# Low parts of weights, reciprocal roots and their neighbours in VectorE's queue

## The chip, the cores and the metric

The kernel runs on one core of a Trainium2 chip. TensorE (PE) multiplies, ScalarE (ACT), VectorE (DVE) and GpSimd (POOL) do the elementwise work, SyncE (SP) issues the transfers. Each engine takes its instructions in one fixed order and waits on semaphores for the others. The metric is the device time of one execution in microseconds (us); of several runs the median stands.

## The reference

Three transformer-like blocks follow each other on one sequence of 512 tokens with 1024 channels, all in float32. Cut to what the change touches:

```
x = first_block(x, ...)     # pooling mixer, LN; dilated attention, LN
x = second_block(x, ...)    # rmsnorm; short conv, sparse attention, gMLP; rmsnorm, residual
x = third_block(x, ...)     # rmsnorm; gated linear attention + conv; rmsnorm; conv FFN; rmsnorm

def layer_norm(x, g, b):    # first block
    return (x - mean(x)) * rsqrt(var(x) + LN_EPS) * g + b

def hybrid_layer(x, ...):   # end of the second block
    out = rmsnorm(merged @ w_out, g_post)
    return x + gate * out

def mixer_merge(o_hg, g, ...):            # third block
    o = rmsnorm_3(o_hg, gn_w) * silu(g)   # per head of 128 channels
    y_hg = o @ w_hg_out
    u = silu(layernorm_3(dwconv1d(u, dw_w, dw_b), ln_w, ln_b))   # the conv norm
    y_cv = u @ w_cv_out
```

## The kernel before, in words

Activations lie channels by tokens: eight tiles of 128 channels by 512 tokens. A float32 product is made of three matmuls on split operands. `w()` (lines 123 to 131) loads a weight tile `wr` of 128x1024 by DMA, ACT copies its high part `wh` (line 129), and an elementwise subtraction gives the low part `wl` (line 130). `prod_a` then runs, for each of eight k, high by high, high by low and low by high (lines 143 to 145). The pool of weight tiles holds three of each kind. The attribute `wlo` says which engine makes the low part; it is set to POOL ahead of several places and back to DVE behind them.

`rsqrt` (lines 209 to 233) computes a reciprocal root by a bit trick and two steps of refinement on a tile of 128x4. On DVE it has ten instructions; with `eng` set to POOL the first one is on DVE and thirteen follow on POOL, since POOL makes each fused step (line 216) from two (lines 219 and 220). Nine roots pass POOL: the layer norm at the end of block 1 and the eight heads of the gated linear attention (gla) in block 3. `bcast_tok` (line 250) spreads a root over 128 partitions by four PE transposes, named `S`.

A scheduler orders each engine's instructions when the kernel is built, from priorities and estimated costs; `high_priority(offset=FIRST)` puts instructions ahead of the others that are ready. The order in the program is then fixed.

The places that matter:

- *End of block 1* (lines 642 to 664): layer norm root on POOL, then a sum of squares on PE, a second root on DVE (`rms_end`), and the modulation into `h2`. Beside it block 3's 256 context tokens are prepared (`cx`, scans at line 1065, transposes `T` at line 1075).
- *End of block 2* (lines 952 to 995): three sums over channels (`sum`, lines 290 and 967) are reduced by matmuls with ones (line 297); a first root, a few small steps `rs_v`, a second root; then per channel tile `acc` times the first root (line 985), plus the residual (line 986), stored, and in a second loop modulated with the second root into `h3`.
- *The gla heads* (`gla_back`, lines 1203 to 1222): output matmuls `O` (1207 to 1209), squares on ACT, a root on POOL, `o` = output times root (1215), four PE transposes `T` (1220).
- *The conv norm* (lines 1301 to 1314): statistics, a root on DVE, then per tile minus mean (1310), times root (1311), SiLU, split. Between them stand the products with `w_hg_out` (line 1307).
- *The halves* (line 322 on): the norm in front of the FFN, done for two halves of the tokens, with sums of squares `ss` (line 290) reduced at line 297.

Of the kernel before, what the change touches and what calls it, by code (L numbers as in the profile page):

```python
# [44 lines left out]
CPOOL = 1  # L45
# [8 lines left out]
class K:  # L54
    def __init__(self, ctx, tc, I):
        self.tc, self.nc, self.I = tc, tc.nc, I
        self.tasks, self.cols = [], {}
        self.wlo = self.nc.vector
        ep = ctx.enter_context
        self.const = ep(tc.tile_pool(name="const", bufs=1))  # L60
        self.wp = ep(tc.tile_pool(name="wp", bufs=3))
        self.big = ep(tc.tile_pool(name="big", bufs=6))
        self.wk = ep(tc.tile_pool(name="wk", bufs=2))
        self.sm = ep(tc.tile_pool(name="sm", bufs=3))
        self.mmp = ep(tc.tile_pool(name="mmp", bufs=3, space=PSUM))
# [57 lines left out]
    def w(self, src, kt, n=P, offset=None):  # L123

        with self.tc.high_priority(offset=offset):
            r = self.wraw(src, kt, n)
            h = self.wp.tile([P, kt, n], F32R, name="wh", tag="wh")
            l = self.wp.tile([P, kt, n], F32R, name="wl", tag="wl")
            self.nc.scalar.activation(h, r, AF.Copy)  # L129
            self.wlo.tensor_sub(l, r, h.bitcast(F32))  # L130
        return h, l
# [77 lines left out]
    def rsqrt(self, v, n, mult, eps, eng=None):  # L209

        e = eng or self.nc.vector

        def fma(out, a, b, y):

            if eng is None:
                e.scalar_tensor_tensor(out, a, b, y, op0=ALU.add, op1=ALU.mult)
            else:
                u = self.small((P, n), "rs_u", bufs=2)
                e.tensor_scalar(u, a, b, 0.0, op0=ALU.add, op1=ALU.add)
                e.tensor_mul(out, u, y)  # L220
        x, y, a, t, xc = (self.small((P, n), "rs_" + c, bufs=2) for c in "xyatc")
        self.nc.vector.tensor_scalar(x, v, mult, eps, op0=ALU.mult, op1=ALU.add)
        e.tensor_scalar(y.bitcast(I32), x.bitcast(I32), -0.5, float(0x5F3759DF), op0=ALU.mult, op1=ALU.add)

        e.tensor_mul(a, y, y)
        e.tensor_scalar(xc, x, -0.5 * 0.375 ** 3, 0.0, op0=ALU.mult, op1=ALU.add)  # L226
        e.tensor_mul(a, a, x)
        fma(t, a, -10.0 / 3, a)
        fma(y, t, 5.0, y)
        e.tensor_mul(a, y, y)  # L230
        e.tensor_mul(a, a, xc)
        fma(y, a, 1.5 * 0.375, y)
        return y
# [27 lines left out]
    def ln_end(self, st, eps, eng=None):  # L261

        mv = self.small((P, NT, 2), "mv4", bufs=1)
        for n in range(NT):
            self.nc.vector.bn_aggr(mv[:, n], st[:, n])
        m = self.bcast_tok(mv[:, :, 0])
        return m, self.bcast_tok(self.rsqrt(mv[:, :, 1], NT, 1.0, eps, eng))
# [52 lines left out]
    def halves(self, src, add, norms, finish, cut, mix):  # L320


        for j in range(cut):
            add(j)
        self.wlo = self.nc.gpsimd
# [84 lines left out]
def block1(k, ctx, w0, acc, x):  # L410
# [6 lines left out]
    for half in range(2):  # L417
        z = None
        for g in (2 * half, 2 * half + 1):
            w = POOL_W[g]  # L420
            k.wlo = nc.gpsimd if g == 1 else nc.vector
# [111 lines left out]
def block1b(k, ctx, acc, h1, x2d):  # L533
# [10 lines left out]
    for j in range(8):  # L544
        k.wlo = nc.gpsimd if j == 0 else nc.vector
# [8 lines left out]
        k.wlo = nc.vector  # L554
# [98 lines left out]
    mean, rstd = k.ln_end(st, LN_EPS, nc.gpsimd)  # L653
# [9 lines left out]
    k.wlo = nc.gpsimd  # L663
# [54 lines left out]
def block2(k, ctx, hT, x2d, x3d):  # L718
# [69 lines left out]
    k.wlo = nc.gpsimd  # L788
    kg = blocks("k"), blocks("v")
    k.wlo = nc.vector  # L790
# [177 lines left out]
    k.wlo = nc.gpsimd  # L968
# [13 lines left out]
    h = k.b16(F32R, name="h3h"), k.b16(F32R, name="h3l")  # L982
    for j in range(8):
        a = acc[:, j]
        nc.vector.tensor_mul(a, a, r)
        nc.vector.tensor_add(a, a, res[:, j])
        nc.sync.dma_start(out=x3d[:, j], in_=a)
    for j in range(8):
        k.modulate(j, acc[:, j], r2, k.cols["A3"], k.cols["B3"], h)
# [134 lines left out]
def gla_back(k, h, hT, V, R, q, tot, masks, gnw, DB, y):  # L1124
# [89 lines left out]
    r = k.rsqrt(ss, NT, 1.0 / P, EPS, nc.gpsimd)  # L1214
# [10 lines left out]
def block3(k, hT, x3d, out):  # L1225
# [49 lines left out]
    k.wlo = nc.gpsimd  # L1275
    run(BEFORE[:5])
    k.wlo = nc.vector
# [22 lines left out]
    k.wlo = nc.vector  # L1300
    yT = k.b16(name="yT")
    mean, rstd = k.ln_end(bst, EPS)
    yc = k.b16(F32R, name="ycvh"), k.b16(F32R, name="ycvl")
    for j in range(8):
# [5 lines left out]
        nc.vector.tensor_sub(c, c, mean)  # L1310
# [40 lines left out]
    for c0, nk in CHUNKS:  # L1351
        ft = k.b16(F32R, shape=(P, 2, 4, S), name="ft")
        for jj in range(nk):
# [14 lines left out]
            if j == CPOOL:  # L1368
                k.wlo = nc.vector
# [169 lines left out]
```

## Time and profile before

| | us |
|---|---|
| median of 3 runs (lowest, highest) | 3197.41 (3193.45, 3418.14) |
| the profiled execution, its own time | 3195.51 |
| its span, first to last instruction | 3193.5 |
| PE busy | 3090.1 (97%) |
| DVE busy | 2052.4 (64%) |
| ACT busy | 1242.9 (39%) |
| POOL busy | 310.8 (10%) |

The busy shares are means over stages with different limits. PE is nearly always busy, so what counts for an edit is whether PE waits at its place, and for whom. The views used are the page's shares, the waits grouped by who ended them, the granted TensorE clock by stretches, and the timelines of single places. A bracket at a timeline row's end gives the idle time before it and who ended it. A tile's name stands without its number, and `x4` at the end of a row means four such instructions in a row.

### The profile page before, as it was taken

What the parts mean: (1) busy time and instruction counts of PE and PEld (TensorE: products, weight loads), DVE (VectorE), ACT (ScalarE), POOL (GpSimd) and SP (SyncE); (2) the same over time, 40 slices, a digit from 0 to 9 for tenths busy, and PEclk for the clock granted to TensorE, in tenths of its full rate; (3) what the DMA queues carried; (4) which work ended last, traced back from release to release, by engine and by line L of the source; (5) the groups of instructions that cost most, each with busy time, mean ns of one, the idle gap of its engine ahead of it and who ended that gap; (6) DMA issues with size and microseconds to landing.
All of it is one profiled execution on the core that took longest, in us unless ns stands there. A gap on an engine that the chain in (4) does not pass through costs nothing.

```text
span 3193.5 us, 44907 instructions
## 1 busy us (share of the span) xinstructions
PE 3090.1 (97%) x17460; PEld 2547.2 (80%) x17460; DVE 2052.4 (64%) x4049; ACT 1242.9 (39%) x2092; POOL 310.8 (10%) x380
## 2 busy tenths in 40 slices
PE   8999999999999899999999999989999998989998
PEld 7888878787877787877778888878877776878886
DVE  8466664656454745555444354589997899688777
ACT  4333544434343433334443223342455462333232
POOL 1400000000000301111100101030010020210000
PEclk9999999999999999999999999999999999999999
DMA  8223343434322421111113222333222224422332
GB/s 289 100 93 132 114 160 112 152 114 146 123 87 71 129 99 66 60 66 66 54 57 106 93 92 93 134 120 112 98 91 69 90 73 142 139 73 93 98 100 80
DMA packets 112773, 334.41 MB, mean 105 GB/s; under 512 B 17584, under 2 KB 22704, under 8 KB 112560
## 3 DMA queue, kind: packets, MB, share of 16 engines
q1 hardware_dynamic: 112560, 331.54, 30.6%
q8 instruction: 137, 2.24, 0.3%
q14 instruction: 76, 0.62, 0.1%
HBM read 316.82 MB, written 14.68 MB: 104 GB/s over the span
## 4 chain that ended last, share of the span: by engine, by line
PE 45%; DVE 6%; ACT 2%; issue 1%; POOL 1%; DVEq 0%; ACTq 0%; POOLq 0%
PE mm L143 12%; PE mm L144 12%; PE mm L145 12%; PE O L885 1%; PE mm L172 1%; PE mm L174 1%; PE mm L173 1%; DVE wl L130 1%; PE S L869 1%; PE T L878 1%; DVE cy L1255 0%; ACT wh L129 0%; PE S L1161 0%; POOL rs_c L226 0%; DVE ss L290 0%
## 5 line engine op out<-in xcount | busy, mean ns | idle before, releaser
L129 ACT ACTIVATE wh<-wr 128x1024 fp32r<-128x1024 f32 (+3 forms) x505 | 504.4, 1000 | 1090.5 <-PE mm L144 823.6
L130 DVE TENSOR_TENSOR wl<-wr,wh 128x1024 fp32r<-128x1024 f32 (+2 forms) x455 | 547.7, 1205 | 436.6 <-ACT wh L129 433.1
L143 PE MATMUL mm<-h2h,wh 128*128 128x512 f32 (+1 forms) x776 | 309.5, 399 | 0.9 <-ACT th L677 0.8
L145 PE MATMUL mm<-h2h,wl 128*128 128x512 f32 (+1 forms) x776 | 309.3, 399 | 0.0
L144 PE MATMUL mm<-h2l,wh 128*128 128x512 f32 (+1 forms) x776 | 309.1, 398 | 0.0
L144 PE MATMUL mm<-h1l,wh 128*128 128x512 f32 x512 | 210.9, 412 | 1.7 <-DVE h1l L318 1.4
L143 PE MATMUL mm<-h1h,wh 128*128 128x512 f32 x512 | 207.0, 404 | 0.6 <-ACT h1h L317 0.6
L145 PE MATMUL mm<-h1h,wl 128*128 128x512 f32 x512 | 207.5, 405 | 0.0
L143 PE MATMUL mm<-h3h,wh 128*128 128x512 f32 x512 | 201.8, 404 | 3.4 <-ACT th L1261 2.2
L144 PE MATMUL mm<-h3l,wh 128*128 128x512 f32 x512 | 201.0, 402 | 1.5 <-DVE h3l L318 1.5
L145 PE MATMUL mm<-h3h,wl 128*128 128x512 f32 x512 | 199.7, 400 | 0.0
L1255 DVE SCALAR_TENSOR_TENSOR cy<-uc,dww,cy 128x512 f32<-128x512 f32 x240 | 177.1, 749 | 3.4
L143 PEld LDWEIGHTS mm<-h2h,wh 128*128 128x128 f32 (+1 forms) x776 | 145.8, 188 | 27.6 <-ACT th L677 1.5
L144 PEld LDWEIGHTS mm<-h2l,wh 128*128 128x128 f32 (+1 forms) x776 | 145.8, 188 | 26.2
L145 PEld LDWEIGHTS mm<-h2h,wl 128*128 128x128 f32 (+1 forms) x776 | 145.7, 188 | 25.3
L130 POOL TENSOR_TENSOR wl<-wr,wh 128x1024 fp32r<-128x1024 f32 (+1 forms) x50 | 118.3, 2370 | 324.7 <-ACT wh L129 324.6
L366 DVE CUSTOM_DVE_ANT_0 gr<-gr,crow 128x256 f32<-128x256 f32 x352 | 135.7, 440 | 9.5 <-DMA gr<-in_w_mod 6.3
L143 PE MATMUL mm<-h4h,wh 128*128 128x512 f32 (+1 forms) x368 | 140.6, 384 | 0.2 <-DVE fc L1366 0.2
L145 PE MATMUL mm<-h4h,wl 128*128 128x512 f32 (+1 forms) x368 | 140.7, 383 | 0.0
L144 PE MATMUL mm<-h4l,wh 128*128 128x512 f32 (+1 forms) x368 | 140.7, 383 | 0.0
L1363 DVE SCALAR_TENSOR_TENSOR fc<-up,fdw,fc 128x512 f32<-128x512 f32 x176 | 131.9, 751 | 4.9
L875 ACT ACTIVATE pe<-sb,nm 128x128 f32<-128x128 f32 (+3 forms) x128 | 71.3, 557 | 119.1 <-DVE nm L872 118.9
(522 smaller groups left out, 7283.9 us busy)
## 6 DMA issues: line engine op xcount, KB each, us to landing
gr<-in_w_mod SPq DMA_DIRECT2D x64, 512.0 KB, 4.8
wr<-in_w_up SPq DMA_DIRECT2D x44, 512.0 KB, 3.5
wr<-in_w_in_a SPq DMA_DIRECT2D x32, 512.0 KB, 3.5
wr<-in_w_f SPq DMA_DIRECT2D x32, 512.0 KB, 3.5
wr<-in_w_v SPq DMA_DIRECT2D x32, 512.0 KB, 3.7
wr<-in_w_in_b SPq DMA_DIRECT2D x32, 512.0 KB, 3.5
wr<-in_w_a SPq DMA_DIRECT2D x32, 512.0 KB, 3.5
gr<-in_w_ada SPq DMA_DIRECT2D x24, 512.0 KB, 4.5
```

What stands on the lines that cost most here:

```text
L129: self.nc.scalar.activation(h, r, AF.Copy)
L130: self.wlo.tensor_sub(l, r, h.bitcast(F32))
L143: mm(ps, lhsT=wh[:, k], rhs=xh[:, k0 + k, tok], start=first and k == 0, stop=False)
L144: mm(ps, lhsT=wh[:, k], rhs=xl[:, k0 + k, tok], start=False, stop=False)
L145: mm(ps, lhsT=wl[:, k], rhs=xh[:, k0 + k, tok], start=False, stop=last and k == kt - 1)
L172: mm(ps, lhsT=sel(xh, k), rhs=wh[:, kk], start=st, stop=False)
L173: mm(ps, lhsT=sel(xh, k), rhs=wl[:, kk], start=False, stop=False)
L174: mm(ps, lhsT=sel(xl, k), rhs=wh[:, kk], start=False, stop=en)
L366: nc.vector.tensor_tensor_reduce(out=r[:, sl], in0=r[:, sl], in1=self.crow[:, sl], scale=1.0, scalar=0.0, op0=ALU.mult, op1=ALU.add, accum ...
L875: nc.scalar.activation(pe, sb, AF.Exp, bias=m, scale=-1.0, accum_out=lt[:, n, b:b + 1])
L1255: nc.vector.scalar_tensor_tensor(c, u[:, t:t + S], dww[:, j, t:t + 1], c, op0=ALU.mult, op1=ALU.add)
L1363: nc.vector.scalar_tensor_tensor(c, u[:, a:a + 8, b:b + 64], fw[:, j, t:t + 1], c, op0=ALU.mult, op1=ALU.add)
```

## The change

All low parts are made on DVE: 50 move there from POOL (20 in block 1's pooling mixer and one in its halves, 10 in the stage around the end of block 1, 12 at the end of block 2, 7 before and in the FFN's start). All reciprocal roots run on DVE, in a section of highest priority, and so do the statistics' last step in `ln_end`. At two places `issue_after` queues passes over whole tiles behind the last instruction of a root, `k.chain`: the products of `acc` with the first root at the end of block 2, behind the second root, and the subtraction of the mean in the conv norm. The two loops at the end of block 2 become one.

```diff
@@ w()
             self.nc.scalar.activation(h, r, AF.Copy)
-            self.wlo.tensor_sub(l, r, h.bitcast(F32))
+            self.nc.vector.tensor_sub(l, r, h.bitcast(F32))
@@ rsqrt
-    def rsqrt(self, v, n, mult, eps, eng=None):
...
+    def rsqrt(self, v, n, mult, eps):
+
+        e = self.nc.vector
         x, y, a, t, xc = (self.small((P, n), "rs_" + c, bufs=2) for c in "xyatc")
...
+        fma = lambda out, a, b, y: e.scalar_tensor_tensor(out, a, b, y, op0=ALU.add, op1=ALU.mult)
+        with self.tc.high_priority(offset=FIRST):
+            e.tensor_scalar(x, v, mult, eps, op0=ALU.mult, op1=ALU.add)
+            e.tensor_scalar(y.bitcast(I32), x.bitcast(I32), -0.5, float(0x5F3759DF), op0=ALU.mult, op1=ALU.add)
+
+            e.tensor_mul(a, y, y)
+            e.tensor_scalar(xc, x, -0.5 * 0.375 ** 3, None, op0=ALU.mult)
+            e.tensor_mul(a, a, x)
+            fma(t, a, -10.0 / 3, a)
+            fma(y, t, 5.0, y)
+            e.tensor_mul(a, y, y)
+            e.tensor_mul(a, a, xc)
+            self.chain = fma(y, a, 1.5 * 0.375, y)
         return y
@@ ln_end
-        for n in range(NT):
-            self.nc.vector.bn_aggr(mv[:, n], st[:, n])
+        with self.tc.high_priority(offset=FIRST):
+            for n in range(NT):
+                self.nc.vector.bn_aggr(mv[:, n], st[:, n])
@@ end of block 1
-    mean, rstd = k.ln_end(st, LN_EPS, nc.gpsimd)
+    mean, rstd = k.ln_end(st, LN_EPS)
@@ end of block 2
     h = k.b16(F32R, name="h3h"), k.b16(F32R, name="h3l")
+    chain = k.chain
     for j in range(8):
         a = acc[:, j]
-        nc.vector.tensor_mul(a, a, r)
+        with k.tc.issue_after(chain.ins):
+            nc.vector.tensor_mul(a, a, r)
         nc.vector.tensor_add(a, a, res[:, j])
         nc.sync.dma_start(out=x3d[:, j], in_=a)
-    for j in range(8):
         k.modulate(j, acc[:, j], r2, k.cols["A3"], k.cols["B3"], h)
@@ gla_back
-    r = k.rsqrt(ss, NT, 1.0 / P, EPS, nc.gpsimd)
+    r = k.rsqrt(ss, NT, 1.0 / P, EPS)
@@ conv norm
     mean, rstd = k.ln_end(bst, EPS)
+    chain = k.chain
...
-        nc.vector.tensor_sub(c, c, mean)
+        with k.tc.issue_after(chain.ins):
+            nc.vector.tensor_sub(c, c, mean)
```

What the scheduler makes of it shows in the order of the instructions. Three places on DVE follow; a row is line, operation, output and inputs, shape.

DVE at the end of block 2, from the second root's first step `rs_x` on (`acc` is the channel tile, `S` the broadcast first root, `x2r` the residual). Before:

```order
L222 TENSOR_SCALAR rs_x<-rs_v 128x4
L986 TENSOR_TENSOR acc_17018<-acc_17018,x2r 128x512
L223 TENSOR_SCALAR rs_y<-rs_x 128x4
L226 TENSOR_SCALAR rs_c<-rs_x 128x4
L985 TENSOR_TENSOR acc_17018<-acc_17018,S 128x512
L225 TENSOR_TENSOR rs_a<-rs_y 128x4
L985 TENSOR_TENSOR acc_17018<-acc_17018,S 128x512
L227 TENSOR_TENSOR rs_a<-rs_a,rs_x 128x4
L986 TENSOR_TENSOR acc_17018<-acc_17018,x2r 128x512
L216 SCALAR_TENSOR_TENSOR rs_t<-rs_a 128x4
L986 TENSOR_TENSOR acc_17018<-acc_17018,x2r 128x512
L216 SCALAR_TENSOR_TENSOR rs_y<-rs_t,rs_y 128x4
```

Now (line 971 is the product of line 985 before):

```order
L213 TENSOR_SCALAR rs_x<-rs_v 128x4
L214 TENSOR_SCALAR rs_y<-rs_x 128x4
L217 TENSOR_SCALAR rs_c<-rs_x 128x4
L216 TENSOR_TENSOR rs_a<-rs_y 128x4
L128 TENSOR_TENSOR wl<-wr,wh 128x1024
L218 TENSOR_TENSOR rs_a<-rs_a,rs_x 128x4
L211 SCALAR_TENSOR_TENSOR rs_t<-rs_a 128x4
L211 SCALAR_TENSOR_TENSOR rs_y<-rs_t,rs_y 128x4
L221 TENSOR_TENSOR rs_a<-rs_y 128x4
L222 TENSOR_TENSOR rs_a<-rs_a,rs_c 128x4
L211 SCALAR_TENSOR_TENSOR rs_y<-rs_a,rs_y 128x4
L971 TENSOR_TENSOR acc_17012<-acc_17012,S 128x512 x2
```

The passes over `acc` that stood between the root's steps have moved behind them; one low part stands inside, made here now and not on POOL.

DVE at the gla head whose `o` has the number 20795 before and 20771 now, from the root's first step to `o`. Before, with only the root's first step on DVE:

```order
L1138 TENSOR_TENSOR KD<-R_18824 128x512
L222 TENSOR_SCALAR rs_x<-ss_20794 128x4
L1119 TENSOR_SCALAR tot<-R_18824 128x4
L1120 SCALAR_TENSOR_TENSOR tot<-R_18824,sp 128x4
L1152 TENSOR_TENSOR E<-R_18824 128x8x64
L130 TENSOR_TENSOR wl<-wr,wh 128x1024 x2
L1215 TENSOR_TENSOR o_20795<-O,rs_y 128x512
L1153 TENSOR_TENSOR E<-R_18824 128x8x64
```

Now, the second half of the root (`rs_t` to the last `rs_y`) and `o` at its end:

```order
L128 TENSOR_TENSOR wl<-wr,wh 128x1024
L211 SCALAR_TENSOR_TENSOR rs_t<-rs_a 128x4
L1138 TENSOR_TENSOR E<-R_18818 128x8x64
L211 SCALAR_TENSOR_TENSOR rs_y<-rs_t,rs_y 128x4
L199 SCALAR_TENSOR_TENSOR sg_20792<-sg_20792,mm 128x512
L221 TENSOR_TENSOR rs_a<-rs_y 128x4
L1137 TENSOR_TENSOR E<-R_18818 128x16x32
L222 TENSOR_TENSOR rs_a<-rs_a,rs_c 128x4
L1140 TENSOR_TENSOR E<-E,q_18821 128x512
L211 SCALAR_TENSOR_TENSOR rs_y<-rs_a,rs_y 128x4
L1138 TENSOR_TENSOR E<-R_18818 128x16x32
L1200 TENSOR_TENSOR o_20771<-O,rs_y 128x512
```

Nearly each step of the root is now followed by another instruction of DVE's line. On PE, between this head's last `O` matmul and its transposes `T`, 25 matmuls of 128x512 stood before, and 39 stand now.

DVE at the conv norm, from the statistics on (`mv` mean and variance, `S` a broadcast). Before:

```order
L259 BN_STATS bst<-T 128x6 x4
L265 BN_AGGR mv_22807<-bst 128x2 x4
L222 TENSOR_SCALAR rs_x<-mv_22807 128x4
L223 TENSOR_SCALAR rs_y<-rs_x 128x4
L226 TENSOR_SCALAR rs_c<-rs_x 128x4
L1310 TENSOR_TENSOR cy<-cy,S 128x512
L130 TENSOR_TENSOR wl<-wr,wh 128x1024
L225 TENSOR_TENSOR rs_a<-rs_y 128x4
L1310 TENSOR_TENSOR cy<-cy,S 128x512
L227 TENSOR_TENSOR rs_a<-rs_a,rs_x 128x4
L1310 TENSOR_TENSOR cy<-cy,S 128x512
L216 SCALAR_TENSOR_TENSOR rs_t<-rs_a 128x4
```

Now, from the root's third instruction on (line 1290 is line 1307 before, 1294 and 1295 are 1310 and 1311):

```order
L217 TENSOR_SCALAR rs_c<-rs_x 128x4
L216 TENSOR_TENSOR rs_a<-rs_y 128x4
L218 TENSOR_TENSOR rs_a<-rs_a,rs_x 128x4
L211 SCALAR_TENSOR_TENSOR rs_t<-rs_a 128x4
L1290 SCALAR_TENSOR_TENSOR yT<-th,mm 128x512
L211 SCALAR_TENSOR_TENSOR rs_y<-rs_t,rs_y 128x4
L221 TENSOR_TENSOR rs_a<-rs_y 128x4
L222 TENSOR_TENSOR rs_a<-rs_a,rs_c 128x4
L211 SCALAR_TENSOR_TENSOR rs_y<-rs_a,rs_y 128x4
L1294 TENSOR_TENSOR cy<-cy,S 128x512 x2
L1295 TENSOR_TENSOR cy<-cy,S 128x512 x2
L1294 TENSOR_TENSOR cy<-cy,S 128x512 x2
```

The subtractions between the steps have moved behind the root. Directly ahead of the statistics DVE's line now has a low part, and PE's line has all 24 matmuls of the last product with `w_hg_out` ahead of the norm's last transposes, where 7 of them came only behind these transposes before.

## Rows read from the trace of the kernel before

**Rows 1.** The page, part 1: busy us (share), instructions.

```profile
PE 3090.1 (97%) x17460; PEld 2547.2 (80%) x17460; DVE 2052.4 (64%) x4049; ACT 1242.9 (39%) x2092; POOL 310.8 (10%) x380
```

**Rows 2.** PE's waits by releaser: us in total, times, longest.

```profile
PE T L1220 <- DVE o L1215: 14.5, 6, 3.8
PE S L250 <- DVE rs_y L216: 14.0, 4, 5.8
PE mm L297 <- DVE ss L290: 11.8, 3, 7.6
PE T L1075 <- ACT cx L1070: 8.7, 4, 4.8
...
PE S L250 <- POOL rs_y L220: 1.8, 1, 1.8
PE mm L297 <- DVE sum L967: 1.7, 1, 1.7
...
PE mm L145 <- POOL wl L130: 1.0, 2, 0.6
```

**Rows 3.** The page, part 5: busy us, mean ns | idle before.

```profile
L130 DVE TENSOR_TENSOR wl<-wr,wh 128x1024 fp32r<-128x1024 f32 (+2 forms) x455 | 547.7, 1205 | 436.6 <-ACT wh L129 433.1
...
L130 POOL TENSOR_TENSOR wl<-wr,wh 128x1024 fp32r<-128x1024 f32 (+1 forms) x50 | 118.3, 2370 | 324.7 <-ACT wh L129 324.6
```

**Rows 4.** Half-clock stretches: us, PE busy, PEclk; the first and the sum.

```profile
1089.00:1095.80 6.80, 5.45 (x26) 0.50 0.23 81
...
sum 80.10, PE 51.34; mean PE 5.70
```

**Rows 5.** Timeline (start, length) of POOL, then DVE, at the context's scans.

```profile
1083.71 5.12 POOL L130 TENSOR_TENSOR wl<-wr,wh 128x1024 fp32r<-128x1024 f32 x2 [2.02 <-ACT wh L129]
...
1083.82 5.56 DVE L1065 TENSOR_TENSOR_SCAN cx<-ones,cx 128x256 f32<-128x256 f32 x2
```

**Rows 6.** Timeline of DVE at block 2's norm; last, PE's broadcast.

```profile
2097.34 0.68 DVE L290 TENSOR_TENSOR sum<-sum,sq 128x512 f32<-128x512 f32 x1
...
2098.27 2.54 DVE L290 TENSOR_TENSOR sum<-sum,sq 128x512 f32<-128x512 f32 x1
2100.73 2.83 DVE L967 TENSOR_TENSOR sum<-sum,xu 128x512 f32<-128x512 f32 x1
...
2105.51 0.16 DVE L222 TENSOR_SCALAR rs_x<-mm 128x4 f32<-128x4 f32 x1 [1.62 <-PE mm L297]
...
2107.10 0.16 DVE L216 SCALAR_TENSOR_TENSOR rs_y<-rs_a,rs_y 128x4 f32<-128x4 f32 x1
...
2111.81 0.17 DVE L222 TENSOR_SCALAR rs_x<-rs_v 128x4 f32<-128x4 f32 x1
...
2116.40 2.37 DVE L216 SCALAR_TENSOR_TENSOR rs_t<-rs_a 128x4 f32<-128x4 f32 x1
...
2123.78 0.15 DVE L216 SCALAR_TENSOR_TENSOR rs_y<-rs_a,rs_y 128x4 f32<-128x4 f32 x1
...
2123.99 1.11 PE L250 MATMUL S<-ident,rs_y 128*128 128x128 f32 x4 [5.17 <-DVE rs_y L216]
```

**Rows 7.** Timeline at the conv norm: the root's broadcast on PE.

```profile
2707.83 1.12 PE L250 MATMUL S<-ident,rs_y 128*128 128x128 f32 x4 [5.78 <-DVE rs_y L216]
```

**Rows 8.** Window: PE, PEld, DVE, ACT, POOL busy, PEclk; one head's timeline.

```profile
2160.00:2700.00 540.00, 513.26 (x4077) 421.41 (x4076) 484.12 (x767) 241.60 (x385) 46.30 (x110) 0.97 0.29 96
...
2469.74 0.16 DVE L222 TENSOR_SCALAR rs_x<-ss 128x4 f32<-128x4 f32 x1
...
2476.18 0.69 DVE L1215 TENSOR_TENSOR o<-O,rs_y 128x512 f32<-128x512 f32 x1 [3.26 <-POOL uc L1250]
...
2471.14 0.39 PE L143 MATMUL mm<-h3h,wh 128*128 128x512 f32 x1
2471.37 0.39 PE L144 MATMUL mm<-h3l,wh 128*128 128x512 f32 x1
```

**Rows 9.** Timeline of DVE at the halves: an add of 256 columns.

```profile
2801.61 2.42 DVE L290 TENSOR_TENSOR ss<-ss,sq 128x256 f32<-128x256 f32 x1 [0.46 <-ACT sq L289]
```

More of the change, by code (lines that the diff above doesn't have):

```diff
@@ L44 @@
 CMOD = 2, 3, 3
-CPOOL = 1
 CUT = slice(0, S // 2), slice(S // 2, S)
@@ L57, in __init__ @@
         self.tasks, self.cols = [], {}
-        self.wlo = self.nc.vector
         ep = ctx.enter_context
@@ L206, in table_after @@
             return self.nc.scalar.preload_act_table_set(name)
-    def rsqrt(self, v, n, mult, eps, eng=None):
[L211 to L220, printed above, removed]
-        x, y, a, t, xc = (self.small((P, n), "rs_" + c, bufs=2) for c in "xyatc")
[L222 to L232, printed above, removed]
+    def rsqrt(self, v, n, mult, eps):
+        e = self.nc.vector
+        x, y, a, t, xc = (self.small((P, n), "rs_" + c, bufs=2) for c in "xyatc")
+        fma = lambda out, a, b, y: e.scalar_tensor_tensor(out, a, b, y, op0=ALU.add, op1=ALU.mult)
[10 more added lines that the diff above has]
+            self.chain = fma(y, a, 1.5 * 0.375, y)
         return y
@@ L259, in ln_stats, with ln_end @@
             self.nc.vector.bn_stats(st[:, n, j], t[:, n])
-    def ln_end(self, st, eps, eng=None):
+    def ln_end(self, st, eps):
         mv = self.small((P, NT, 2), "mv4", bufs=1)
-        for n in range(NT):
-            self.nc.vector.bn_aggr(mv[:, n], st[:, n])
+        with self.tc.high_priority(offset=FIRST):
+            for n in range(NT):
+                self.nc.vector.bn_aggr(mv[:, n], st[:, n])
         m = self.bcast_tok(mv[:, :, 0])
-        return m, self.bcast_tok(self.rsqrt(mv[:, :, 1], NT, 1.0, eps, eng))
+        return m, self.bcast_tok(self.rsqrt(mv[:, :, 1], NT, 1.0, eps))
     def rms_add(self, ps, j, x):
@@ L324, in halves @@
             add(j)
-        self.wlo = self.nc.gpsimd
         ws = [self.w(src[j], KT) for j in range(cut, 8)]
@@ L420, in block1 @@
             w = POOL_W[g]
-            k.wlo = nc.gpsimd if g == 1 else nc.vector
             pg = k.b16(F32R, shape=(P, 2, 4, S), name="pg")
@@ L544, in block1b @@
     for j in range(8):
-        k.wlo = nc.gpsimd if j == 0 else nc.vector
         if j % 2 == 0:
@@ L553, in block1b @@
         nc.vector.tensor_copy(V[0][:, :, (j % 2) * P:(j % 2 + 1) * P], tps)
-        k.wlo = nc.vector
         if j % 2 == 0:
@@ L662, in block1b @@
     h = k.b16(F32R, name="h2h"), k.b16(F32R, name="h2l")
-    k.wlo = nc.gpsimd
     k.steps(ctx, "r")
@@ L787, in values @@
         VV.append(t)
-    k.wlo = nc.gpsimd
     kg = blocks("k"), blocks("v")
-    k.wlo = nc.vector
     values(0)
@@ L967, in block2 @@
             nc.vector.tensor_add(xu, xu, t)
-    k.wlo = nc.gpsimd
     k.steps(ctx, "s")
@@ L1274, in run @@
             {"c": lambda: conv(n), "v": lambda: value(n), "g": lambda: gate(I["w_gcv"], n, gcd), "h": lambda: gate(I["w_ghg"], n, ghd)}[it[0]]()
-    k.wlo = nc.gpsimd
     run(BEFORE[:5])
-    k.wlo = nc.vector
     run(BEFORE[5:])
@@ L1299, in block3 @@
         t[1]()
-    k.wlo = nc.vector
     yT = k.b16(name="yT")
     mean, rstd = k.ln_end(bst, EPS)
+    chain = k.chain
     yc = k.b16(F32R, name="ycvh"), k.b16(F32R, name="ycvl")
@@ L1367, in block3 @@
             k.split(ft[:, 0, jj], ft[:, 1, jj], c2)
-            if j == CPOOL:
-                k.wlo = nc.vector
             for _ in range((0, 2, 3, 3)[jj] if nk == 4 else (2, 6)[jj]):
```

## The prediction

> **What bounds the kernel now.** I read the page's shares first: the reader sees TensorE (PE) busy for 3090.1 of 3193.5 us [rows 1], so at most 103 us of the span are PE standing idle. Then PE's waits, grouped by who ended them [rows 2]: they say in which places that idle time lies, and nearly all the long ones end on a small VectorE (DVE) or GpSimd (POOL) result of a norm: the transposes of a head's normalised output (14.5 us in 6 waits), broadcasts of a reciprocal root (14.0 and 1.8 us), the ones-matmuls on a sum of squares (11.8 and 1.7 us), and the transposes of the context block (8.7 us). Then the granted clock by stretches [rows 4]: nine stretches, 80.1 us together, ran at 0.50 (1.2 of 2.4 GHz); a matmul takes twice as long there, so they cost PE about 40 us on top. The row shown follows a gap of 5.17 us before a broadcast [rows 6]. Idle time and clock loss are together some 140 us, 4% of the run: that is all the change can win, since it removes no matmul.
>
> The timelines of DVE and POOL show how the two disturb each other. Beside two weight low parts on POOL (5.12 us) a pair of DVE scans over 256 columns takes 5.56 us [rows 5], though a pass over 512 columns takes 0.68 [rows 6]. In block 2's norm a sum of squares takes 2.54 us, the next add 2.83 and one step of the root 2.37 [rows 6].
>
> **The low parts.** A low part takes 2370 ns on POOL and 1205 ns on DVE [rows 3], so 50 moved parts load DVE with 60 us and free it of the stalls. PE waited only 1.0 us for POOL's low parts in the whole run [rows 2], so the 21 of them in block 1 are worth nothing: matmuls in plenty hide them (I let -1 to 0 stand). The other 29 lie at norms.
>
> *Block 1's last norm and the context block.* The root on POOL costs a wait of 1.8 us [rows 2]; on DVE ten steps take 1.8 us (2105.51 to 2107.26 [rows 6]) where the first and POOL's thirteen had to finish, so -1.8. The scans' stall (5.56 less two passes of 0.68, 4.2 us) lies in the longest wait for the context block, 4.8 us [rows 2]: -4.2. A half-clock stretch of 6.8 us [rows 4] follows it; its loss is 3.4 us and I take half, -1.7. Against that, six low parts (7.2 us), five of them moved, now stand on DVE ahead of the second root; PE has context matmuls ahead of it and I charge +1. Sum -7, bounds -10 (the stretch goes, the parts are hidden) and -3 (the gap only moves).
>
> *Block 2's norm.* The two slow adds lose 1.9 and 2.1 us against 0.68 [rows 6], but two low parts of 1.2 us stand ahead of them now: -1.6 of the 1.7 us wait [rows 2]. The second root ran from 2111.81 to 2123.93, 12.1 us for ten steps, with passes and stalls between [rows 6]; in the new order a single low part stands inside it, so about 1.8 + 1.2 = 3 us. The 5.17 us wait of its broadcast [rows 6] goes. Two half-clock stretches of 6.8 us lie in this place; I let one go, -3.4. Charged against: the eight passes that ran between the root's steps come behind it, and so DVE needs four passes (2.4 us at a spacing of 0.6) for each of the eight h3 tiles against nine matmuls of 0.23 us [rows 8], 2.1 us, for which PE waits: 8 x 0.3, +3. Sum -7, bounds -13 (both stretches, no wait for h3) and -3.
>
> What a drop of the clock hangs on is weighed here. The rows show it at 0.50 after a gap and at full level before. The Trainium skill (Perfetto Trace Analysis, Matmul Optimizations) says that the matmul engine scales its power with utilisation, so that matmuls should run back to back. By that rule every shortened gap could give its stretch back as well, which is the third rival below; by the rows I count one and a half stretches here and above.
>
> **The roots on DVE.** *The eight gla heads.* A POOL root ended DVE's wait for the head's output in most heads and PE's 14.5 us stand behind it [rows 2]. In the head of 2469 us the output came 6.4 us after the root's first step, after an idle DVE of 3.26 us [rows 8], and PE waited 3.8. The diff asks for the head of the queue, but the new order has another instruction between nearly all steps: seven passes of 0.6, a low part of 1.2 and the small steps, about 6.5 us. So the output comes no sooner. What changes is PE's line: 39 matmuls of 512 columns instead of 25 stand between the head's last output matmul and its transposes, 14 x 0.23 = 3.2 us more cover. Counted so over all eight heads, with 0.6 us for a pass and 1.2 for a low part between the steps, the chains grow by an estimated 10 us and the cover by 16; set against each other head by head, they leave waits of about 9.6 us where 14.5 were. So -5. Two half-clock stretches of this stage go in half the cases and new ones come as easily. Bounds: -12 (both stretches and most waits go) and +5 (waits as now, the DVE load on top).
>
> Against this part speaks DVE's load in this stage: 484 of 540 us, 90% [rows 8]. The Trainium skill (Perfetto Trace Analysis, Optimizing Scalar/DVE Operations) advises the opposite of this change: where DVE is saturated, move work off it, to ScalarE or even GpSimd, though it adds that DVE and GpSimd share a read port and a move between them may not help. By that rule this term would be a loss, the slow rival; by the waits on POOL in the rows it is a small gain.
>
> **The passes behind the root, conv norm.** Seven subtractions of 0.6 us stood between the root's steps and let PE wait 5.78 us for the broadcast [rows 7]. In the new order only one pass is inside. But PE now runs all matmuls of the stage's last group before the norm's transposes, so it has none left to do during statistics and root; a low part that waits for the weight copy stands ahead of the statistics on DVE (+1.2); and the first normalised tile has three more passes ahead of it (+1.2 to +1.8) while the wait itself shrinks by about one. I take +2, bounds 0 and +3. The half-clock stretch stays.
>
> **The halves before the FFN.** The longest wait on a sum of squares, 7.6 us [rows 2], has three stalls like the 2.42 us add of 256 columns [rows 9]; each loses at least 1.7 us, and each is replaced by a low part of 1.2: -2, bounds -4 and 0.
>
> Sum: -7 -7 -5 +2 -2 = -19 us against the profiled execution's 3195.5, so 3176.5; the median of the runs shown lies 1.9 above that execution: **3178 us**. The bounds add to -40 and +2.
>
> **The rivals.**
> - *Nothing gained* (chance 0.18): PE is 97% busy and each wait that goes is met by the next one (h3, the second root, the statistics). For it: the conv norm shows just that in the order. Against: the stalls beside POOL are plain in the rows. The gains of 1.8, 1.7 and some others stay, the new waits eat them: about 3195.
> - *The in-order DVE becomes the bound in the gla stage* (0.13): one mechanism, the head's chain of steps queued between passes, and low parts at DVE's head that wait for ScalarE. If PE's cover is used up by earlier waits, the 10 us by which the chains grow stand on PE's line in full: waits of 14.5 + 10 us, and four more heads with a half-clock stretch of 6.8 us, 4 x 3.4 = 14. That is +24 in this stage; with +3 at the conv norm and -16 elsewhere +11, so 3208, slower than before. It decides once the outputs come over 2 us after the cover ends in most heads.
> - *The clock stays up* (0.15): if the gaps in the norms fall short of what precedes a drop, seven of the nine stretches can go (not the one of 2382 us nor the last, at places that the change leaves alone): five of 6.8 and two of 10.2 us give 27 us, of which 5 are in the sum: -41, so 3156.
> - The forecast's own case has 0.54. That the change doesn't do what it says at the gla heads (the root isn't at the head of the queue) is already in it.
>
> **Range and chances.** The own case covers about 3165 to 3190; taking in "nothing gained" above and "clock stays up" below, 3153 to 3204 holds about eight in ten; the slow rival stays mostly outside. A measurement of this kernel can tell some 2%, 64 us, from no change. Faster by that needs nearly half of all idle and clock loss: 0.03. Slower by that needs six times the slow rival's loss: 0.01. Within: 0.96.
>
> **What would show it.** In the changed profile: no low part and no root on POOL (118 us of its busy time gone with the low parts alone), DVE's share up by about a point; the scans and the sums of squares at their own lengths; the broadcast of block 2's second root with no PE wait, and short waits for h3 in its place; the waits for the heads' transposes at 8 to 12 us in all; the conv norm's wait still 5 to 7 us; six to eight half-clock stretches. The prediction is wrong if the waits for the heads' transposes exceed 20 us, if PE waits for low parts on DVE by more than 5 us in all, or if half-clock stretches number four or fewer.

## The result

The changed kernel takes **3158.2 us** (median of four runs, 3156.05 to 3160.26) against 3193.95 before (median of 3197.41, 3193.45 and 3193.95; a fourth run, of 3418.14 us, was in a slow state and is left out). The ratio is 0.9885 with a 95% interval of 0.9866 to 0.9904. The change is faster by 35.8 us, 1.1%, well clear of the runs' spread and inside the 2% to which the prediction gave 0.96. The forecast was 3178. The sign was right and the time lies inside the range of 3153 to 3204, but outside the own case (3165 to 3190): the gain is nearly twice the sum of 19 us.

### The profile page after: what moved, and what is told of

It reads as the page before. It is cut to its first block, busy times and chain, and to the rows that moved or that the text cites. A ratio compares the mean times of both kernels' runs of the same rounds, so it can differ in the third digit from the quotient of the medians.

```text
span 3156.8 us, 44898 instructions
## 1 busy us (share of the span) xinstructions
PE 3082.8 (98%) x17460; PEld 2540.7 (80%) x17460; DVE 2052.1 (65%) x4180; ACT 1245.3 (39%) x2092; POOL 150.0 (5%) x222
## 4 chain that ended last, share of the span: by engine, by line
PE 46%; DVE 6%; ACT 1%; issue 1%; DVEq 0%; ACTq 0%
PE mm L142 13%; PE mm L141 13%; PE mm L143 13%; PE O L870 1%; DVE wl L128 1%; PE mm L171 1%; PE mm L170 1%; PE mm L172 1%; PE S L854 1%; PE T L863 1%; DVE cy L1240 0%; PE S L1146 0%; ACT wh L127 0%; PE S L1185 0%; PE S L921 0%
## 5 line engine op out<-in xcount | busy, mean ns | idle before, releaser
L128 DVE TENSOR_TENSOR wl<-wr,wh 128x1024 fp32r<-128x1024 f32 (+3 forms) x505 | 601.6, 1193 | 456.7 <-ACT wh L127 450.5
L357 DVE CUSTOM_DVE_ANT_0 gr<-gr,crow 128x256 f32<-128x256 f32 x352 | 131.6, 426 | 11.2 <-DMA gr<-in_w_mod 5.8
L141 PEld LDWEIGHTS mm<-h3h,wh 128*128 128x128 f32 x512 | 95.8, 189 | 26.4 <-ACT h3h L309 3.6
```

The source lines that it names most:

```text
L128: self.nc.vector.tensor_sub(l, r, h.bitcast(F32))
L141: mm(ps, lhsT=wh[:, k], rhs=xh[:, k0 + k, tok], start=first and k == 0, stop=False)
L357: nc.vector.tensor_tensor_reduce(out=r[:, sl], in0=r[:, sl], in1=self.crow[:, sl], scale=1.0, scalar=0.0, op0=ALU.mult, op1=ALU.add, accum ...
```

## The profile after

The page's first part, beside [rows 1]:

```profile
PE 3082.8 (98%) x17460; PEld 2540.7 (80%) x17460; DVE 2052.1 (65%) x4180; ACT 1245.3 (39%) x2092; POOL 150.0 (5%) x222
```

The span is 3156.8 us (3193.5 before), so PE is idle for 74.0 us instead of 103.4. DVE took over 50 low parts and nine POOL roots and is busy no longer than before: 2052.1 against 2052.4. The groups of DVE instructions whose number did not change take 55 us less in all. The page's group of low parts shows them all on one engine, at 1193 ns, and none on POOL [rows 3]:

```profile
L128 DVE TENSOR_TENSOR wl<-wr,wh 128x1024 fp32r<-128x1024 f32 (+3 forms) x505 | 601.6, 1193 | 456.7 <-ACT wh L127 450.5
```

So what DVE gained in work it lost in stalls. PE's waits by releaser (total, times, longest), to be read beside [rows 2]:

```profile
PE mm L289 <- DVE ss L282: 9.3, 3, 5.0
PE S L241 <- DVE rs_y L211: 4.5, 4, 2.0
PE mm L141 <- DVE kg L733: 4.1, 1, 4.1
...
PE mm L755 <- ACT hs L750: 2.0, 1, 2.0
...
PE T L1205 <- DVE o L1200: 1.3, 2, 0.8
...
PE T L1060 <- ACT cx L1055: 1.0, 1, 1.0
```

The heads' transposes fell from 14.5 us to 1.3, root broadcasts from 14.0 to 4.5, context transposes from 8.7 to 1.0. Among the waits that are new or longer, two count below: a copy kg (4.1, new) and a hidden state hs (2.0, where the longest was 0.6). Half-clock stretches of the changed kernel (length, PE busy and count, PEclk), three of eight and the sum, beside [rows 4]:

```profile
1106.60:1113.40 6.80, 5.47 (x13) 0.50 0.19 66
...
2369.50:2372.90 3.40, 2.86 (x15) 0.51 0.00 0
...
2669.90:2683.60 13.70, 8.51 (x21) 0.50 0.38 117
...
sum 53.30, PE 33.59; mean PE 4.20
```

In such a stretch matmuls of 512 columns start 0.43 us apart, outside it 0.23 (both at 1103 to 1110 us of the changed kernel). So a stretch costs half of PE's busy time in it: 33.59 / 2 = 16.8 us now, 51.34 / 2 = 25.7 before. Idle time -29.4 and clock -8.9 make -38.3; the span fell by 36.7.

**Where it came from.** The PE instruction of the same number (of 17460) begins earlier or later by the times below (the kernel's trace minus that of before, us; a column is what one place adds). A is block 1's last norm and context, B block 2's norm, then the eight gla heads, C the conv norm, H the halves. The last four rows are experiments of the next section.

| | start to B (of it A) | B | gla heads | C | H | rest |
|---|---|---|---|---|---|---|
| forecast | -7 (-7) | -7 | -5 | +2 | -2 | |
| after | -4.8 (-2.2) | -8.4 | -22.7 | +0.7 | -2.0 | +0.4 |
| e1, low parts alone | -0.8 | -5.5 | -1.9 | +1.2 | -2.1 | 0.0 |
| e2, roots alone | -1.9 | +3.3 | -20.5 | +3.2 | +0.3 | +0.1 |
| e4, heads' roots on POOL | -5.0 | -8.4 | -2.1 | -2.2 | -2.2 | -0.1 |
| e8, earlier transposes | -3.9 | -8.4 | -3.8 | -2.2 from C to the end | | |

Nearly all the surprise lies in one place, the gla heads. Their stage before, from the start of [rows 8] to the table's bound, and the same work in the changed kernel (busy PE, PEld, DVE, ACT, POOL, then PEclk):

```profile
2160.00:2692.00 532.00, 505.35 (x4041) 415.06 (x4040) 477.11 (x756) 240.54 (x384) 46.30 (x110) 0.97 0.28 95
...
2147.00:2656.00 509.00, 495.97 (x4039) 408.54 (x4038) 478.63 (x824) 241.88 (x384) 4.47 (x14) 1.00 0.30 99
```

DVE is busy for 94% of the stage against 90%, with nearly the same work (478.6 us against 477.1) in a shorter stage. The half-clock stretches of the stage before the change were these, where after has the one of 2369.50 us shown above:

```profile
2382.60:2396.30 13.70, 10.84 (x96) 0.50 0.21 77
2474.80:2481.60 6.80, 4.67 (x16) 0.50 0.21 70
2526.00:2532.80 6.80, 5.93 (x16) 0.50 0.50 178
```

Half of their busy time is 10.7 us, of after's 1.4: -9.3. All PE idle time of the stage (between the table's bounds, PE instructions 11400 and 15300) fell from 26.7 to 13.0 us: -13.7. Together -23.0, against the -22.7 of the table.

The -9.3 has two parts. The stretches of 6.8 us lie around two of the heads' waits and are gone with them: -5.3. The stretch of 13.7 us lies at the second head, whose transposes did not wait before either. It lies around two other waits, before:

```profile
2383.26 0.80 PE L1209 MATMUL O<-SS,QI 128*128 128x128 f32 x2 [3.85 <-DVE SS L1203]
...
2390.10 0.79 PE L143 MATMUL mm<-h3h,wh 128*128 128x512 f32 x1 [2.21 <-ACT th L1261]
```

Both waits stay, of 3.30 and 2.20 us now, but the stretch is 3.4 us instead of 13.7: -4.0. The last section shows that this length varies behind the same waits, so these 4.0 us are luck as far as the runs can tell.

One head of the changed kernel, the one of [rows 8]: DVE from the root's first step to the output (a "..." stands for passes, low parts and other steps without idle time), then PE's transpose.

```profile
2451.07 0.16 DVE L213 TENSOR_SCALAR rs_x<-ss 128x4 f32<-128x4 f32 x1
...
2452.78 1.22 DVE L128 TENSOR_TENSOR wl<-wr,wh 128x1024 fp32r<-128x1024 f32 x1
2453.92 0.15 DVE L211 SCALAR_TENSOR_TENSOR rs_t<-rs_a 128x4 f32<-128x4 f32 x1
...
2457.29 0.68 DVE L1200 TENSOR_TENSOR o<-O,rs_y 128x512 f32<-128x512 f32 x1
```

```profile
2458.40 0.60 PE L1205 MATMUL T<-ident,o 128*128 128x128 f32 x4
```

The output comes 6.2 us after the first step, where it was 6.4: as forecast, no sooner. But DVE works on through those 6.2 us, where it had stood idle for 3.26, and PE arrives without a wait, where it had waited 3.8. Before, the root of this head was itself held up on POOL. Its first step there took 2.98 us beside DVE's passes and low parts, while later steps took about 0.2:

```profile
2470.00 2.98 POOL L223 TENSOR_SCALAR rs_y<-rs_x 128x4 int32<-128x4 int32 x1 [51.29 <-DVE rs_x L222]
2473.05 0.19 POOL L226 TENSOR_SCALAR rs_c<-rs_x 128x4 f32<-128x4 f32 x1
```

So the collision goes both ways.

In block 2's norm, beside [rows 6], two sums of squares, the add after them and the second root:

```profile
2090.78 1.28 DVE L282 TENSOR_TENSOR sum<-sum,sq 128x512 f32<-128x512 f32 x2
...
2094.05 0.68 DVE L952 TENSOR_TENSOR sum<-sum,xu 128x512 f32<-128x512 f32 x1
...
2104.80 0.16 DVE L213 TENSOR_SCALAR rs_x<-rs_v 128x4 f32<-128x4 f32 x1
...
2107.61 0.16 DVE L211 SCALAR_TENSOR_TENSOR rs_y<-rs_a,rs_y 128x4 f32<-128x4 f32 x1
```

```profile
2107.92 0.62 PE L241 MATMUL S<-ident,rs_y 128*128 128x128 f32 x4 [0.28 <-DVE rs_y L211]
```

All adds run at 0.64 to 0.68 us, the root takes 3.0 us instead of 12.1, and its broadcast waits 0.28 us instead of 5.17.

## The experiments

Theory: what the gla heads gain comes from their roots leaving POOL, by way of DVE's idle time, of the work that the scheduler puts ahead of PE's transposes, and of the clock; block 2 gains from the stalls that POOL's low parts cause; the two orders that the diff asks for (steps at the head of the queue, passes behind the root) are secondary. Rivals: the low parts did it; cover on PE did it alone; the asked-for order did it. Every ratio is to the kernel before on the same chip (3193.8 to 3195.7 us).

**e1: only the 50 low parts.**

```diff
-            self.wlo.tensor_sub(l, r, h.bitcast(F32))
+            self.nc.vector.tensor_sub(l, r, h.bitcast(F32))
```

> The kernel before with one part alone: all 50 low parts on DVE, roots and loops as before. Theory (the heads' roots carry the gain of 37 us: 22 to 23 us in the gla stage, since the scheduler puts 307 instead of 239 matmuls of 512 columns between the eight heads' last output matmuls and their transposes): the gla stage stays as before, waits of PE for the heads' output 12 to 15 us; gained are 2.5 us in block 1, some at the end of block 1, 3 to 6 at the end of block 2 and 2 at the halves, in all 8 to 13 us: 3182 to 3188. Rival (the stalls beside POOL's low parts carry most of it): 25 us and more, 3170 or less.

3183.2 us, ratio 0.9965 [0.9952, 0.9978], as expected. The heads' transposes still wait 14.4 us in 6 waits. The low parts are not what the heads gained from; the new wait for kg is already here (2.9 us).

**e2: only the roots**, as in the change, on the kernel before with its low parts on POOL.

```diff
-    r = k.rsqrt(ss, NT, 1.0 / P, EPS, nc.gpsimd)
+    r = k.rsqrt(ss, NT, 1.0 / P, EPS)
```

> The kernel before with one part alone: all roots on DVE in the section of highest priority, the low parts on POOL and the passes as before. Theory (the heads' roots carry it): cover of 307 matmuls as in the changed kernel, PE's waits for the heads' output under 3 us instead of 14.5, no half-clock stretch at the heads of 2475 and 2526 us, 22 to 25 us gained: 3170 to 3174. Rival (the low parts carry it): under 10 us, 3186 or more.

3179.93 us, ratio 0.9953 [0.9938, 0.9968]: the total missed its range, the parts tell why. The heads give -20.5, but block 2 loses 3.3 us. The second root's broadcast there, PE's timeline:

```profile
2121.69 1.11 PE L243 MATMUL S<-ident,rs_y 128*128 128x128 f32 x4 [5.14 <-DVE rs_y L213]
```

The root, though asked to the head of DVE's queue, takes 11.6 us (12.1 before). Passes over acc still stand between its steps, and three of the steps take 2.1 to 2.3 us while POOL has low parts. Low parts alone give 10.6 us of median (same batch, 3193.79), roots alone 13.9, together 24.5 of 35.8. The other 11 appear only in the whole change. By the table they lie mostly in B (-8.4 where the two parts give -5.5 and +3.3) and in C. In B the place at the head of the queue is not worth much beside POOL's low parts. The whole change has the single loop at block 2's end too, which neither part has and no run takes back; its share is not shown.

**e4: the change, with the heads' roots alone back on POOL.**

```diff
-    r = k.rsqrt(ss, NT, 1.0 / P, EPS)
+    r = k.rsqrt_pool(ss, NT, 1.0 / P, EPS, nc.gpsimd)
```

> The changed kernel with one part undone: the eight heads' roots on POOL again. Theory (heads' roots): cover back to 239 matmuls, waits for the heads' output 12 to 15 us again, 18 to 23 us of the 37 lost: 3176 to 3181. Rival (the rest of the change makes the gain and the heads' order doesn't matter): lost at most 5 us, 3163 or less.

3176.61 us, ratio 0.9946 [0.9929, 0.9962], as expected: 18.4 us lost by one line. PE's wait, and DVE's wait in two heads:

```profile
PE T L1231 <- DVE o L1226: 14.5, 6, 3.8
```

```profile
2403.52 0.69 DVE L1226 TENSOR_TENSOR o<-O,rs_y 128x512 f32<-128x512 f32 x1 [3.50 <-POOL rs_y L237]
...
2460.98 0.69 DVE L1226 TENSOR_TENSOR o<-O,rs_y 128x512 f32<-128x512 f32 x1 [3.26 <-POOL uc L1261]
```

The waits are back to the tenth. (In the second row the releaser shown is POOL's next work after the root.) Half-clock stretches are back too, behind three of the six waits:

```profile
2461.50:2464.90 3.40, 3.17 (x10) 0.50 0.03 5
2601.50:2604.90 3.40, 3.40 (x40) 0.50 0.02 5
2635.60:2639.00 3.40, 3.40 (x11) 0.50 0.61 215
```

Half of their busy time is 5.0 us, near the 5.3 of the two stretches before.

**e7: before, with the heads' transposes at a lower priority**, so that the scheduler puts more matmuls ahead of them (291 of 512 columns over the eight heads where 239 stood; 307 in the change), the roots left on POOL.

```diff
-        nc.tensor.transpose(tps[:, c], o[:, c], k.ident)
+        with k.tc.high_priority(offset=-30):
+            nc.tensor.transpose(tps[:, c], o[:, c], k.ident)
```

> The kernel before, roots of the heads on POOL, with one edit: the heads' four transposes have a priority lowered by 30. In the order that puts 47, 39 and 45 matmuls in place of 19, 25 and 35 behind the third, fourth and fifth head's last output matmul; the other heads keep their 20, 18, 55, 47 and 20. Theory (the cover on PE decides, not the engine of the root): the waits of 1.4, 3.8 and 2.9 us at these three heads go, and the two half-clock stretches at 2475 and 2526 us with them (6.8 us at most), while the waits of 1.8, 2.5 and 2.0 us at the first, seventh and eighth head stay: 8 to 14 us gained, 3182 to 3188. Rival (the root on POOL itself is what costs, with DVE idle and PE's later work late behind it): under 3 us, 3193 or more.

3191.03 us, ratio 0.9991 [0.9981, 1.0]: missed, nearly nothing gained. PE's waits:

```profile
PE T L1221 <- DVE o L1215: 8.7, 4, 2.5
...
PE S L1161 <- DVE E L1155: 3.2, 1, 3.2
```

```profile
2472.41 0.69 DVE L1215 TENSOR_TENSOR o<-O,rs_y 128x512 f32<-128x512 f32 x1 [2.72 <-POOL uc L1251]
```

In two of the three heads the wait for the output went, but DVE still stood idle ahead of it (the row shows one), and behind one of the two the next product from DVE, E, was late by 3.2 us instead. More cover on PE alone gained 2.8 us of median and in part moved the gap.

**e8: the change, with the cover taken back in three heads** (39 matmuls of 512 columns to 25 in the head shown above). AHEAD holds, for each head, how many matmuls may stand ahead of its transposes.

```diff
+            with self.tc.issue_after(self.lastT.ins):
+                return self.nc.tensor.matmul(*args, **kw)
...
+        k.ahead = AHEAD[j]
         run(BESIDE[j])
```

> The changed kernel (roots on DVE) with the cover on PE taken back at three heads: matmuls traced behind a head are queued behind its transposes, so that the fourth, fifth and eighth head have 25, 26 and 31 matmuls of 512 columns behind their last output matmul in place of 39, 50 and 42; the other five keep 42, 24, 24 to 26, 50 and 36. Theory (the later place of the transposes is what takes the waits away): waits of about 2.5, 6 and 2.5 us come up at these three heads (14, 24 and 11 matmuls of 0.227 us less than the little slack there), with one or two half-clock stretches, 9 to 18 us lost: 3167 to 3176. Rival (a DVE that no longer stands idle ahead of the heads' output is what counts, the place of the transposes is not): at most 4 us lost, 3162 or less.

3177.09 us, ratio 0.994 [0.9925, 0.9955], 1 us beyond the expected range: as much lost as in e4, with the roots on DVE. PE's waits; the second, of 4.9 us at 2510 us, is at the transposes of one of the three heads (the profile names a product of ScalarE as what ended it):

```profile
PE S L1153 <- DVE E L1147: 5.2, 3, 2.6
PE T L1212 <- ACT KI L1176: 4.9, 1, 4.9
```

PE's idle time in the stage is 23.4 us (13.0 in the change) and the half-clock time 23.9 (3.4), which by half of PE's busy time is 10.2 us against 1.4: nearly half of the loss is clock. Not all of the loss belongs to the three heads. In the traces some 7 of the 18.9 us come ahead of the first of them: 3.8 by a stretch of 13.7 us at the second head, where the change has 3.4, the rest around a wait of 2.6 us for E at 2390 us, which the change does not have. Some 12 us are left at the three heads. e7 and e8 together: the heads' gain needs both, the root on the engine that uses it and enough work ahead of PE's transposes.

**e3: the change without the two orders "passes behind the root".**

```diff
-        with k.tc.issue_after(chain.ins):
-            nc.vector.tensor_mul(a, a, r)
+        nc.vector.tensor_mul(a, a, r)
...
-        with k.tc.issue_after(chain.ins):
-            nc.vector.tensor_sub(c, c, mean)
+        nc.vector.tensor_sub(c, c, mean)
```

> The changed kernel without the two queueings behind a root. In the order the second root of block 2 has four passes and two low parts more between its steps, and the conv norm's root six subtractions. Theory (the queueing shortens the roots that PE waits for): about 4 us longer at the one, of which PE has cover for some, and 3 us at the other, where the changed kernel with its passes behind the root waited 1.99 us and the kernel with roots alone 4.88: 3 to 7 us lost, 3161 to 3166. Rival (the passes must be done anyhow and only move): within 1.5 us.

3159.6 us, ratio 0.9884 [0.987, 0.9899]: no effect, as the rival had it. At the conv norm the broadcast waits 4.9 us again where the change has 2.0, yet C as a whole adds only 1.5 us more (+2.2 against +0.7), which is within what two traces differ by.

**e5: the change with the roots at their ordinary priority.**

```diff
-        with self.tc.high_priority(offset=FIRST):
+        if True:
```

> The changed kernel with the roots (and the statistics' last step) at normal priority. The order then puts 66 us of other DVE work instead of 53 between the heads' first root step and their output, and 391 matmuls instead of 307 between their last output matmul and their transposes. Theory (what counts is that the scheduler knows when the output comes and puts the transposes behind enough matmuls; the place at the head of the queue is not needed): PE's waits for the heads' output stay under 3 us, the time within 6 us of the changed kernel: 3153 to 3164. Rival (only the highest priority brings the output in time): waits over 8 us, 3167 or more.

3158.6 us, ratio 0.988 [0.9863, 0.9896]: no effect, as expected. **e12** takes e3 and e5 together, so that only the engines change (and the two loops at block 2's end stay one):

> The changed kernel without highest priority for the roots and without the two queueings: only the engines are changed. Each of the two taken away alone cost 0 to 1 us. Theory (the engines of low parts and roots carry all of the gain): 3156 to 3163. Rival (the two replace each other, and without both the roots of block 2 and of the conv norm come late): 3165 to 3172.

3160.07 us, ratio 0.9893 [0.9877, 0.9909]. The heads have even more matmuls ahead of their transposes then (391). The engines give the result; the asked-for order carries nothing that these runs can measure.

**e11: the change with the 12 low parts at block 2's end back on POOL.**

```diff
+    k.wlo = nc.gpsimd
...
+    k.wlo = nc.vector
```

> The changed kernel with the 12 low parts at the end of block 2 on POOL again, the roots on DVE. Theory (low parts on POOL and a root on DVE disturb each other: with roots alone the second root's broadcast waited 5.14 us as before, so the two parts of the change need each other here): stalls of 2 us in the sums and the root come back, the waits on sums and broadcast with them, and the place ends 8 to 12 us later than in the changed kernel: 3166 to 3170. Rival (the root's shorter queue alone repairs the place, what POOL does beside it is hidden): at most 3 us, 3161 or less.

3166.88 us, ratio 0.9913 [0.9895, 0.993], as expected: block 2 goes from -8.4 to +1.5. DVE's timeline there:

```profile
2091.46 2.53 DVE L283 TENSOR_TENSOR sum<-sum,sq 128x512 f32<-128x512 f32 x1
2093.92 2.83 DVE L953 TENSOR_TENSOR sum<-sum,xu 128x512 f32<-128x512 f32 x1
...
2106.16 2.27 DVE L223 TENSOR_TENSOR rs_a<-rs_a,rs_c 128x4 f32<-128x4 f32 x1
```

The slow adds and a slow root step as in [rows 6] come back with POOL's low parts, to 0.1 us, though the root, which was on DVE before too, now stands at the head of its queue.

**e9: the change with the kg copies first in their queues**, for the new wait at A.

```diff
+                        with k.tc.high_priority(offset=FIRST):
```

> The changed kernel with the copies of the compressed keys' blocks (kg, 16 on DVE, 16 on ACT) in the section of highest priority, ahead of the low parts and high parts of weights. Theory (the wait of 4.06 us for kg at 1104 us and the half-clock stretch of 6.8 us behind it have taken the place of the waits for the context block, because low parts that wait for ACT now stand at the head of DVE's line): the wait falls under 2 us, 3 to 6 us gained, 3152 to 3155. Rival (the copies wait for each other, DVE on ACT and back, whatever stands between them): 0 to 1 us gained.

3160.61 us, ratio 0.9889 [0.9874, 0.9904]: the wait stays at 4.1 us, nothing is gained, as the rival had it. The copies alternate between DVE and ScalarE, and their place in the queues is not what holds them. That they wait for each other, the rival's reason, is not shown by this.

**e10: the change with the halves' last adds first in the queue**, for the longest wait left.

```diff
+        with k.tc.high_priority(offset=FIRST if w else 0):
```

> The changed kernel with the residual adds and the adds of squares of the halves in front of the FFN in the section of highest priority; in the order the last residual add then stands ahead of six instructions, a low part among them, and the last add of squares behind four fewer. Theory (the 5.04 us wait on that sum is DVE's queue, 3 us of it instructions that could come later): 1 to 3 us gained, 3155 to 3157. Rival (the sum waits for ACT's squares and PE, not for DVE's queue): within 0.7 us.

3157.83 us, ratio 0.9884 [0.9869, 0.9898]. The wait fell from 5.0 to 3.9 us; in the time it can't be told, as the rival had it. **e13** joins what did no harm: ordinary priority, only the conv norm's passes queued, the halves' adds first.

> A version that may beat the changed kernel: low parts and roots on DVE, roots at normal priority, only the conv norm's passes queued behind their root, and the halves' adds in the section of highest priority. Theory (each of these was worth 0 to 3 us by itself and they lie in different places): 3151 to 3157. Rival (the order around them shifts as much as they give): 3157 to 3162.

3156.13 us (3155.42 to 3157.97), ratio 0.9879 [0.9864, 0.9894]: the lowest median, not to be told from the change. With 391 matmuls ahead of the transposes PE waits 5.4 us for yT at 2644 us, behind the last head. e5 and e12, with the same 391, have this wait too; the change doesn't.

## Why the prediction was right and wrong

**The step that failed is the term for the eight gla heads**, -5 where the stage gave -22.7. Its mechanism held: no idle DVE in the chain, the output no sooner after the first step, more matmuls on PE. Its sizes did not.
- "They leave waits of about 9.6 us where 14.5 were": 1.3 were left. I had let the chains grow by 10 us and the cover by 16. Summed over the heads, the time from the first step to the output went from 54.7 to 61.3 us. What lies ahead of the first step, which I had left as it was, got shorter: from the squares to the first step 2.2 us instead of 5.3, from PE's last output matmul to the end of the squares 13.0 instead of 16.3. So the output came as late as before after PE's last output matmul (76.3 us before, 76.5 after), while PE's cover, the time of its work from there to the transposes, grew from 71.3 to 82.5, by 11.2. I had set a growth of the chain against the cover that the part ahead of the chain took back. e4 and e8 show each side: without the one or the other most of the gain is gone.
- "Two half-clock stretches go in half the cases and new ones come as easily": both went, and none came behind the heads' transposes. I counted 0, it was -5.3. The other -4.0 of the stage's clock, at the second head, is luck that I had not counted either. In the change, e2 and e3 the heads' waits went and the stage gained 20 to 23 us; in e4 and e8, where waits came back, 19 to 21 us of it went, in e8 nearly half by the clock. So a wait on PE that goes should be priced with the half-clock stretch behind it. Not one for one: in e1 and e4 the heads' waits are the old ones, and behind them were three stretches of 3.4 us instead of two of 6.8. But half of PE's busy time in them was nearly the same: 5.3 us before, 5.1 in e1, 5.0 in e4.
- Against the term spoke DVE's load. The Trainium skill (Perfetto Trace Analysis, Optimizing Scalar/DVE Operations) says that moving work off a saturated DVE, even to GpSimd, may make sense, and that a move between these two might not help. As a warning against this change the first part fails here: DVE's share rose from 90% to 94% and the stage became shorter. What PE waited for was DVE's idle time ahead of one instruction.

**A, block 1's last norm and the context:** -7 forecast, -2.2 measured. The gain itself was larger than my outer bound: by the 5700th PE instruction, at 1092 us, the lead had grown by 12.1 us. 9.9 were given back at two places that the prediction didn't name, DVE's copies kg and then hs on ScalarE. The copies and the matmul behind them:

```profile
1106.03 3.55 DVE L733 COPY kg<-mm 64x248 f32<-64x248 f32 x8
```

```profile
1107.93 0.77 PE L141 MATMUL mm<-h2h,wh 128*128 128x512 f32 x1 [4.06 <-DVE kg L733]
```

The stretch of 6.8 us above lies around this wait. That kg is late with low parts on DVE, e1 shows (2.9 us); that its priority isn't the cause, e9. In e5, e12 and e13, where the roots have ordinary priority, the wait is 2.9 us as in e1, so the roots' place at the head of the queue goes with 1.2 of the 4.1. What holds the copies for the rest was not settled.

**B, block 2's norm:** -7 forecast, -8.4 measured, by the forecast mechanism: stalls gone, root in 3.0 us as estimated. I charged 3 us for late h3 tiles; the longest wait for them is 1.5 us, as before. e11 shows that the low parts on POOL are the cause.

**C, the conv norm:** +2 forecast, +0.7 measured. The broadcast, which had waited 5.78 us [rows 7], waits 2.0, but the wait for the first normalised tile (2.85), for the statistics (1.1) and for the transposes (1.7) stay or come, and the half-clock stretch is 13.7 us where it was 10.2. My 5 to 7 us for the broadcast was wrong; that the sum was near is luck.

**H, the halves:** -2, and -2.0 measured; the longest wait went from 7.6 to 5.0 us. **Low parts of block 1:** -2.6 where I let -1 to 0 stand. The runs with all low parts of block 1 on DVE are 2.2 to 3.8 us ahead by 118 us, e2 and e7 without that 0.6 to 1.2. The two waits for POOL's low parts [rows 2] were at 99 and 106 us; there the runs gain 1.6 to 1.7 us, more than the waits' 1.0. What they gain ahead of that, e2 and e7 have in part, so it does not come from the low parts alone.

**The reading of the whole.** "About 40 us on top" for the clock was too much: half of PE's busy time in the stretches is 25.7 us. The rival of the clock staying up gave 3156, near the measured time, for another reason: of its 27 us (19.8 by half of PE's busy time in the seven stretches) the clock gave 8.9; the waits gave 29.4. The slow rival (a bound DVE) fell, and so did "nothing gained". What the prediction named as its refutation, half-clock stretches of four or fewer, did not occur: there are eight, most of them shorter.

## What to carry to other kernels

A small chain between an engine and the matmul engine is priced by three things together: whether the engine that consumes it idles for it, how much work the scheduler puts ahead of the waiting matmuls, and the half-clock stretch behind the wait; each of the first two alone gained little here (3.8 us of the stage in e8, 3.3 in e7). Two changes that touch the same collision can't be priced apart (10.6 and 13.9 us alone, 35.8 together). A busy share of 94% on an engine that is not the bound says little; its idle time ahead of the one instruction that is waited for says much.

## What the runs showed of the hardware that was not expected

The length of a half-clock stretch varies behind the same waits. At the second gla head two waits follow each other in the change:

```profile
2368.58 0.49 PE L1194 MATMUL O<-SS,QI 128*128 128x128 f32 x2 [3.30 <-DVE SS L1188]
...
2374.57 0.50 PE L141 MATMUL mm<-h3h,wh 128*128 128x512 f32 x1 [2.20 <-ACT th L1246]
```

In e5 they are 3.29 and 2.20 us long. The change's stretch, of 2369.50 us, is shown with the profile after; that of e5, and what follows it (length, PE busy, PEclk):

```profile
2369.00:2382.70 13.70, 10.35 (x85) 0.50 0.19 73
2382.70:2386.00 3.30, 3.30 (x105) 1.00 0.06 16
```

13.7 us against 3.4; in e3, e11, e12 and e13 it was 6.8, in e9 and e10 10.2. By half of the busy time that is 5.2 us against 1.4. A stretch can also come where other kernels have none. In e9's trace the clock fell at 585 us, far ahead of what e9 changes, behind a wait of 1.24 us, while PE was then busy without a gap:

```profile
585.00:595.20 10.20, 10.20 (x29) 0.50 0.18 60
```

That is 5.1 us. The same PE instruction waits 0.79 us in e5, and no stretch follows. No run here shows the cause of either; it limits what two profiles of this kernel can tell apart to some 5 us at one place.
